# One more Strassen pair in the gate and up projections, their early sums taken once, and a third of the low halves made by an adding DMA

## The chip, the cores and the metric

The kernel runs on one core of a Trainium2 chip. The metric is the device time of one execution in microseconds (us), lower being better. TensorE (PE in the profile) multiplies, VectorE (DVE), ScalarE (ACT) and GpSimd (POOL) work on tiles in the on-chip memory, and SyncE (SP) issues the loads of the weights.

## The reference, cut to what matters

The reference is two transformer blocks in float32 on 256 tokens of width 2048, one after the other. The first has a differential attention beside a retention, a cross attention over 256 memory tokens, and a gated feed-forward part; the second has a gated spatial part beside a linear recurrence, and a convolved feed-forward part. The change touches the feed-forward part of the first block alone:

```
hf = rmsnorm(x, norm_ffn_g)                                    # (256, 2048)
x = x + (silu(hf @ w_gate) * (hf @ w_up)) @ w_down             # w_gate, w_up: (2048, 5632)
```

## The kernel before, in words

All products are made in three passes, since TensorE works on a shortened float32: each operand is written as hi + lo, where hi is the shortened value and lo the rest, and `mm3` (L190 to L195) issues hi·hi, hi·lo and lo·hi, three matmuls of 128x512. The helper `split` (L173) makes the two parts of a weight: ACT casts the raw weight `w` to `wh` (L175), DVE subtracts `wh` from `w` to get `wl` (L176).

Weights come from HBM in units of 1 MB (a tile `w` of 128x2048, three buffers, loaded by SP at L277). The list `seq` fixes the order of the units, `push` (L282) splits one piece of a unit, and `half` keeps up to five pieces split ahead of TensorE. The pieces `wh` and `wl` of 128x1024 have five buffers each, so a cast has to wait until TensorE has done with an older piece. The compiler of the language then sets the order of the instructions on each engine itself; the source fixes only what depends on what.

Gate and up are computed together by `gemm_q` (L413): 11 groups g of 512 columns, in three parts (PARTS: 4, 4 and 3 groups), each part followed by its share of `w_down`. The 2048 rows of the weights are 16 tiles of 128, taken as eight pairs; one unit `w` holds a pair for gate and up, four blocks of 128x512 (two of gate, then two of up in reversed order). With the tokens split in two halves of 128, one pair is a 2x2 by 2x2 product of blocks. KINDS says how each of the eight pairs u is computed:

- "N": eight products `mm3`, from two pieces (0 and 1) of 1024 columns. DVE makes one `wl` a piece.
- "S": seven products in Strassen's way (the variant of Winograd), from four pieces: "a" is the first half of the unit, "b" and "d" are sums of blocks that DVE makes first (L305 for "b"; L309 and L310 for "d"), "c" is the single block 2 of 512 columns, whose hi and lo go to ordinary tiles `r`.

Before, KINDS is "NSNSNSNN": three S pairs, five N pairs. The sums of the activations that S needs are made once for all groups by the class `Quad` (L103).

The products add up in seven banks of PSUM, M[1] to M[7]. M[2], M[3], M[4] and M[5] take the four buffers of the pool `pg`, M[1], M[6] and M[7] three of the four of the pool `pp`. M[1], M[6] and M[7] get products from S pairs alone. When no S pair is left, gemm_q calls `early` (L843): ACT copies M[1] to the tile m (L844), DVE adds M[6] to give u2 (L845) and M[7] to give u3 (L846). The call stands at the end of the loop over u (`if "S" not in ks[u + 1:]`), so with this KINDS it is made after u = 5, after u = 6 and after u = 7.

After a group, DVE takes the four banks out: M[2] + m (L853), M[4] + u3 (L855), M[5] twice (L857, L858), M[3] (L859); ACT applies SiLU to the first two (L854, L856), and L860 and L861 multiply. The next group needs the same four buffers, so its first products wait for these reads.

Of the kernel before, what the change touches and what calls it, by code (L numbers as in the profile page):

```python
# [8 lines left out]
F32 = mybir.dt.float32  # L9
F32R = mybir.dt.float32r  # L10
I32 = mybir.dt.int32
AF = mybir.ActivationFunctionType
ALU = mybir.AluOpType
# [4 lines left out]
S = 256  # L18
# [3 lines left out]
LN_EPS = 1e-5  # L22
LOOKAHEAD = 4
PARTS = [(0, 4), (4, 8), (8, 11)]
KINDS = "NSNSNSNN"
TAIL = 5


# [18 lines left out]
def tile_kernel(ctx, tc, x, xT, mem, memT, par, alibi, rdecay, ident_d, bc_rows, gm_wsT,  # L47
# [3 lines left out]
    V, A, T, G = nc.vector, nc.scalar, nc.tensor, nc.gpsimd  # L51
# [13 lines left out]
    def nm(s):  # L65
        cnt[0] += 1
        return f"{s}_{cnt[0]}"
# [4 lines left out]
    def rt():  # L72
        return tpool.tile([P, 2, S], F32R, tag="t", name=nm("r"))

    def flat(f):
        return f.rearrange("p a b -> p (a b)")
# [69 lines left out]
    def gps():  # L146
        return psg.tile([P, 512], F32, tag="g", name=nm("pg"))

    def sps():
        return pss.tile([P, 512], F32, tag="p", name=nm("pp"))  # L150
# [22 lines left out]
    def split(hi, lo, src, gcol=None):  # L173
        if gcol is None:
            A.copy(hi, src)  # L175
            V.tensor_tensor(lo, src, hi.bitcast(F32), ALU.subtract)  # L176
        else:
            A.activation(hi, src, AF.Identity, scale=gcol)
            V.scalar_tensor_tensor(lo, src, gcol, hi.bitcast(F32), ALU.mult, ALU.subtract)
# [11 lines left out]
    def mm3(out, lh, rh, start, stop):  # L191

        T.matmul(out, lhsT=lh[0], rhs=rh[0], start=start, stop=False)  # L193
        T.matmul(out, lhsT=lh[0], rhs=rh[1], start=False, stop=False)  # L194
        T.matmul(out, lhsT=lh[1], rhs=rh[0], start=False, stop=stop)  # L195
# [42 lines left out]
    seq = [(w_in_f, 0, u) for u in range(2)]  # L238
# [25 lines left out]
    def kind(w, u):  # L264
        return KINDS[u] if w is w_gu else "N"


    pieces = [(w, g, u, i) for w, g, u in seq for i in ((0, 1) if kind(w, u) == "N" else "acbd")]
    raws, last, sums = [], [None], {}

    def fetch():
        w, g, u = seq[pos[0]]
        raw = wraw.tile([P, 2048], F32, tag="w", name=nm("w"))
        n = 2 if pos[0] == 0 else 1
        for i in range(n):
            c = slice(2048 // n * i, 2048 // n * (i + 1))
            last[0] = nc.sync.dma_start(out=raw[:, c], in_=w[g, u][:, c])  # L277
        raws.append(raw)
        pos[0] += 1

    def push():

        w, g, u, i = pieces[pos[1]]
        if not raws:
            fetch()
        raw = raws[0]
        if i in (1, "d"):
            raws.pop(0)
        pos[1] += 1
        if pos[1] > len(pieces) - TAIL:  # L290

            hi, lo = [flat(rt()) for _ in range(2)], [flat(rt()) for _ in range(2)]
            for k in range(2):
                split(hi[k], lo[k], raw[:, 1024 * i + 512 * k:1024 * i + 512 * k + 512])
        else:
            if i == "c":
                hi, lo = flat(rt()), flat(rt())
            else:
                hi = whi.tile([P, 1024], F32R, tag="h", name=nm("wh"))
                lo = wlo.tile([P, 1024], F32R, tag="l", name=nm("wl"))  # L300
            b = raw.rearrange("p (b n) -> p b n", n=512)
            if i == "a":

                sums["b"] = wsum.tile([P, 2, 512], F32, tag="t", name=nm("wt"))
                V.tensor_tensor(sums["b"], b[:, 3:4, :].to_broadcast([P, 2, 512]), b[:, 0:3:2, :], ALU.subtract)  # L305
            if i == "c":

                d = sums["d"] = wsum.tile([P, 2, 512], F32, tag="t", name=nm("wt"))
                V.tensor_tensor(d[:, 0, :], sums["b"][:, 0, :], b[:, 2, :], ALU.subtract)  # L309
                V.tensor_tensor(d[:, 1, :], d[:, 0, :], b[:, 1, :], ALU.add)  # L310
            if i in ("b", "d"):
                src = sums.pop(i).rearrange("p b n -> p (b n)")
            else:
                src = raw[:, {0: slice(0, 1024), 1: slice(1024, 2048), "a": slice(0, 1024),
                              "c": slice(1024, 1536)}[i]]
            split(hi, lo, src)
        feed.append((w, g, u, i, hi, lo))

    def half(w, g, u, i, n):
# [11 lines left out]
    def tick():  # L331
        for g in list(bg):
            try:
                next(g)
            except StopIteration:
                bg.remove(g)
# [8 lines left out]
    def need(lst, i):  # L345
        while lst[i] is None:
            assert bg
            tick()
        return lst[i]
# [60 lines left out]
    def gemm_q(wap, g, acts, sums_done):  # L410

        M = [None] * 8
        n = len(acts)
        ks = [kind(wap, u) for u in range(n)]
        total = {m: sum(1 if k == "S" else 2 if m in (2, 3, 4, 5) else 0 for k in ks) for m in range(1, 8)}
        done = [0] * 8

        def prod(m, a, b):  # L420
            if M[m] is None:
                M[m] = gps() if m in (2, 3, 4, 5) else sps()
            done[m] += 1
            mm3(M[m], a, b, done[m] == 1, done[m] == total[m])

        for u in range(n):
            a = need(acts, u)
            if ks[u] == "N":
                plan = [(0, [(2, 0, 0, 0), (2, 0, 1, 1), (4, 1, 0, 0), (4, 1, 1, 1)]),
                        (1, [(5, 1, 1, 0), (5, 1, 0, 1), (3, "D", 1, 0), (3, "D", 0, 1)])]  # L430
                for i, ops in plan:
                    hi, lo = half(wap, g, u, i, 512)
                    for m, t, k, b in ops:
                        prod(m, a.diff(k) if t == "D" else a.blk(k, t), (hi[b], lo[b]))
                    tick()
            else:
                plan = [("a", [(1, a.blk(0, 0), 0), (2, a.blk(1, 0), 1)]),
                        ("c", [(3, a.sums(3), 0)]),
                        ("b", [(5, a.sums(0), 0), (7, a.sums(2), 1)]),
                        ("d", [(6, a.sums(1), 0), (4, a.blk(1, 1), 1)])]  # L440
                for i, ops in plan:
                    hi, lo = half(wap, g, u, i, 512)
                    for m, x, b in ops:
                        prod(m, x, (hi[b], lo[b]))
                    if i in "cd":
                        tick()
            if "S" not in ks[u + 1:]:
                sums_done(M)
        return M

    def evac_fm(ps, r):
# [29 lines left out]
    def add_x(ps, g):  # L481
        for t in range(2):
            V.tensor_tensor(xs(t, g), xs(t, g), ps[t], ALU.add)
# [329 lines left out]
    for g in range(4):  # L813
        add_x(gemm_tm(w_xo, g, xo), g)
        spawn(next_in(g, hf_a, sqf, cols("norm_ffn_g", 0, 16), None, KINDS), 1)

# [21 lines left out]
    for g0, g1 in PARTS:  # L838
        acts = [None] * (2 * (g1 - g0))
        for g in range(g0, g1):  # L840
# [7 lines left out]
            M = gemm_q(w_gu, g, hf_a, early)  # L848
# [236 lines left out]
    for g in range(2):  # L1085
        ps = gemm_tm(w_in2_t, g, h2_a)
        u = []
# [161 lines left out]
```

## Time and profile before

| what | value |
|---|---|
| time, median of 3 runs (lowest to highest) | 2601.64 us (2598.96 to 2602.27) |
| profiled execution, its time | 2601.45 us |
| its span, first to last instruction | 2599.7 us |
| mean granted clock of TensorE | 0.997 |
| DVE busy over the span | 69% |
| ACT busy over the span | 53% |
| POOL busy over the span | 2% |
| weight units of gate and up | 88, the first issued at 755.7 us, the last at 1418.9 us |
| DMA, mean over the span | 189 GB/s |

The profile's engine times are unions of busy time; a matmul is listed with its whole passage (0.39 us for 128x512), but the next one starts 0.22 to 0.23 us after it, so the distance of two starts says what a matmul costs. Groups are listed as: line, engine, operation, out<-in by the program's names, shapes, count, then busy time in all, mean ns of one, idle time of the engine before them. The view of the waits lists who waited for whom: us in total, times, longest.

### The profile page before, as it was taken

The numbers are of one execution on the slowest core, as the hardware profiler recorded it, in microseconds if no ns is written. First come the engines' busy times: TensorE is split into PE (matmuls) and PEld (weight loads), VectorE is DVE, ScalarE is ACT, GpSimd is POOL, SyncE is SP. The second block draws the span as 40 slices with busy tenths as digits, with TensorE's granted clock in tenths as the row PEclk, the third lists the DMA queues.
The fourth block names the chain that finished last, engine by engine and source line by source line (L and its number), as shares of the span: only waits on it lengthen the run. The fifth ranks groups of instructions, "written<-read, shape, count | busy, mean of one in ns | idle before, by whom it ended". The sixth has DMA issues, their size and how long they took to land.

```text
span 2599.7 us, 32474 instructions
## 1 busy us (share of the span) xinstructions
PE 2567.3 (99%) x12823; PEld 2172.7 (84%) x12823; DVE 1789.2 (69%) x2284; ACT 1381.7 (53%) x1882; POOL 39.0 (2%) x41
## 2 busy tenths in 40 slices
PE   8999999999999999999999999999999999999998
PEld 7888888888887878878887888888888888888887
DVE  7666566556579885888588767866777745777754
ACT  6555554454466553555355555755555534555543
POOL 1000010000000000000000000000000000000000
PEclk9999999999999999999999999999999999999999
DMA  7455555554454555455555555555555555555563
GB/s 257 162 179 211 201 201 189 194 178 162 146 188 168 196 193 194 178 206 196 193 182 180 205 208 192 178 192 181 188 185 193 184 193 192 194 185 188 189 213 132
DMA packets 72727, 490.58 MB, mean 189 GB/s; under 512 B 8192, under 2 KB 8320, under 8 KB 14592
## 3 DMA queue, kind: packets, MB, share of 16 engines
q1 hardware_dynamic: 72576, 488.52, 53.1%
q8 instruction: 100, 1.64, 0.2%
q14 instruction: 51, 0.42, 0.0%
HBM read 486.39 MB, written 2.10 MB: 188 GB/s over the span
## 4 chain that ended last, share of the span: by engine, by line
PE 94%; DVE 3%; issue 1%; ACT 1%; DMA 0%; SPq 0%; POOL 0%; ACTq 0%; POOLq 0%; DVEq 0%
PE pg L362 24%; PE pg L193 17%; PE pg L195 17%; PE pg L194 17%; PE pg L366 12%; PE pp L193 2%; PE pp L195 2%; PE pp L194 2%; DVE wl L176 1%; PE pp L186 1%; ACT wh L175 1%; DVE wt L305 0%; DVE f L845 0%; DVE f L846 0%; DMA w<-in_w_in_f_dram 0%
## 5 line engine op out<-in xcount | busy, mean ns | idle before, releaser
L176 DVE TENSOR_TENSOR wl<-w,wh 128x1024 fp32r<-128x1024 f32 x866 | 1059.6, 1225 | 665.7 <-ACT wh L175 662.0
L175 ACT CAST wh<-w 128x1024 fp32r<-128x1024 f32 x866 | 909.2, 1051 | 863.9 <-PE pg L195 583.9
L193 PE MATMUL pg<-wh,r 128*128 128x512 f32 x2059 | 798.6, 392 | 12.7 <-DVE f L855 11.2
L194 PE MATMUL pg<-wl,r 128*128 128x512 f32 x2059 | 804.6, 391 | 0.0
L195 PE MATMUL pg<-wh,r 128*128 128x512 f32 x2059 | 802.3, 390 | 0.0
L362 PE MATMUL pg<-r,wh 128*128 128x512 f32 x2688 | 714.9, 395 | 11.4 <-ACT wh L175 7.0
L362 PEld LDWEIGHTS pg<-r,wh 128*128 128x128 f32 x2688 | 471.0, 189 | 86.2 <-ACT wh L175 7.0
L193 PEld LDWEIGHTS pg<-wh,r 128*128 128x128 f32 x2059 | 387.2, 188 | 98.3 <-DVE f L855 14.7
L195 PEld LDWEIGHTS pg<-wh,r 128*128 128x128 f32 x2059 | 387.6, 188 | 80.7
L194 PEld LDWEIGHTS pg<-wl,r 128*128 128x128 f32 x2059 | 387.8, 188 | 80.4 <-DVE wl L176 1.1
L366 PEld LDWEIGHTS pg<-r,wl 128*128 128x128 f32 x2688 | 391.2, 190 | 41.7
L366 PE MATMUL pg<-r,wl 128*128 128x256 f32 x2688 | 406.0, 282 | 0.0
L454 ACT COPY f<-pg 128x256 f32<-128x256 f32 x168 | 60.7, 374 | 88.7 <-PE pg L362 88.7
L175 ACT CAST wh<-wt 128x1024 fp32r<-128x1024 f32 x66 | 69.6, 1055 | 55.3 <-DVE wt L310 21.2
L455 DVE TENSOR_TENSOR f<-pg,f 128x256 f32<-128x256 f32 x168 | 68.9, 420 | 43.7 <-ACT f L454 43.7
L176 DVE TENSOR_TENSOR wl<-wt,wh 128x1024 fp32r<-128x1024 f32 x66 | 80.3, 1219 | 11.9 <-ACT wh L175 11.2
L1112 DVE SCALAR_TENSOR_TENSOR f<-f,pr,f 128x255 f32<-128x255 f32 x192 | 79.9, 479 | 0.0
L456 DVE TENSOR_TENSOR f<-f,rows 128x512 f32<-128x512 f32 x84 | 58.1, 692 | 3.4 <-ACT rows L231 0.8
L1109 ACT ACTIVATE f<-f,pr 128x256 f32<-128x256 f32 x96 | 52.6, 594 | 12.6 <-DVE f L456 12.5
L175 ACT CAST r<-f 128x512 fp32r<-128x512 f32 (+1 forms) x72 | 43.0, 598 | 13.7 <-DVE f L456 8.7
L193 PE MATMUL pp<-wh,r 128*128 128x512 f32 x127 | 49.6, 395 | 0.0
L195 PE MATMUL pp<-wh,r 128*128 128x512 f32 x127 | 49.5, 390 | 0.0
(192 smaller groups left out, 1354.0 us busy)
## 6 DMA issues: line engine op xcount, KB each, us to landing
w<-in_w_up_dram SPq DMA_DIRECT2D x96, 1024.0 KB, 4.7
w<-in_w_down_dram SPq DMA_DIRECT2D x92, 1024.0 KB, 4.7
w<-in_w_gu_dram SPq DMA_DIRECT2D x88, 1024.0 KB, 4.8
w<-in_w_in_t_dram SPq DMA_DIRECT2D x40, 1024.0 KB, 4.8
w<-in_w_in_f_dram SPq DMA_DIRECT2D x39, 1024.0 KB, 4.7
w<-in_w_o_dram SPq DMA_DIRECT2D x16, 1024.0 KB, 4.8
w<-in_w_xk_dram SPq DMA_DIRECT2D x16, 1024.0 KB, 4.8
w<-in_w_xv_dram SPq DMA_DIRECT2D x16, 1024.0 KB, 4.7
```

Of the source, the lines that this page charges most:

```text
L175: A.copy(hi, src)
L176: V.tensor_tensor(lo, src, hi.bitcast(F32), ALU.subtract)
L193: T.matmul(out, lhsT=lh[0], rhs=rh[0], start=start, stop=False)
L194: T.matmul(out, lhsT=lh[0], rhs=rh[1], start=False, stop=False)
L195: T.matmul(out, lhsT=lh[1], rhs=rh[0], start=False, stop=stop)
L362: T.matmul(ps[m], lhsT=hi[k][:, m * P:(m + 1) * P], rhs=ops[k].both(k % 2), start=begin and k == 0, stop=stop, skip_group_check=True)
L366: T.matmul(ps[m][:, S:], lhsT=lo[k][:, m * P:(m + 1) * P], rhs=ops[k].hi(k % 2), start=False, stop=False, skip_group_check=True)
L454: A.copy(f[:, m, :], ps[m][:, S:])
L455: V.tensor_tensor(f[:, m, :], ps[m][:, 0:S], f[:, m, :], ALU.add)
L456: V.tensor_tensor(f, f, bc2(need(r, 0)), ALU.mult)
L1109: A.activation(y[:, j, :], z[:, j, :], AF.Identity, scale=col("ffn_conv_w_2", 192 + c), bias=col("ffn_conv_b_2", c))
L1112: V.scalar_tensor_tensor(y[:, j, d:], z[:, j, :S - d], col("ffn_conv_w_2", 96 * (2 - d) + c), y[:, j, d:], ALU.mult, ALU.add)
```

## The change

Four edits, all in the code of gate and up. The line numbers of the changed kernel are one higher from the constant ADDED on (`split` at L176 and L177, the sums at L306, L310 and L311) and six higher behind `push` (`early` at L850 to L852, taking out at L859 to L867).

1. KINDS goes from "NSNSNSNN" to "SNSNSNSN": a fourth pair is computed with seven products. The pairs S now stand first, and u = 0, 2, 4, 6.
2. The pieces of an S pair come in the order a, b, d, c instead of a, c, b, d. The raw unit is thus read until the last piece.
3. `early` is called only behind an S pair, so once in a group (after u = 6) instead of three times.
4. The second piece of the N pairs u = 1, 3, 5 (ADDED) gets its lo in another way: ACT casts hi, ACT then writes -hi to `wl`, and POOL issues a DMA that reads the same 512 KB of weights from HBM again and adds them onto `wl`. DVE does nothing for it. That is 33 adding DMAs, 3 in each of 11 groups.

```
-KINDS = "NSNSNSNN"
+KINDS = "SNSNSNSN"
+ADDED = (1, 3, 5)
...
-    pieces = [(w, g, u, i) for w, g, u in seq for i in ((0, 1) if kind(w, u) == "N" else "acbd")]
+    pieces = [(w, g, u, i) for w, g, u in seq for i in ((0, 1) if kind(w, u) == "N" else "abdc")]
...
-        if i in (1, "d"):
+        if i in (1, "c"):
             raws.pop(0)
...
-            if i == "c":
+            if i == "b":
                 d = sums["d"] = wsum.tile([P, 2, 512], F32, tag="t", name=nm("wt"))
...
-            split(hi, lo, src)
+            if i == 1 and w is w_gu and u in ADDED:
+                A.copy(hi, src)
+                A.activation(lo, hi.bitcast(F32), AF.Identity, scale=-1.0)
+                G.dma_start(out=lo, in_=w[g, u][:, 1024:2048], accum_op=ALU.add)
+            else:
+                split(hi, lo, src)
...
                 plan = [("a", [(1, a.blk(0, 0), 0), (2, a.blk(1, 0), 1)]),
-                        ("c", [(3, a.sums(3), 0)]),
                         ("b", [(5, a.sums(0), 0), (7, a.sums(2), 1)]),
-                        ("d", [(6, a.sums(1), 0), (4, a.blk(1, 1), 1)])]
+                        ("d", [(6, a.sums(1), 0), (4, a.blk(1, 1), 1)]),
+                        ("c", [(3, a.sums(3), 0)])]
...
-                    if i in "cd":
+                    if i in "bc":
                         tick()
-            if "S" not in ks[u + 1:]:
-                sums_done(M)
+                if "S" not in ks[u + 1:]:
+                    sums_done(M)
```

The first place is DVE at the end of the first group (g = 0), from the read of M[2] on; pg_1244 and pg_1245 are M[2] and M[4], pg_1248 is M[5]. Before:

```order
689 L853 TENSOR_TENSOR f_1323_7039<-pg_1244_6682,f_1239_6675 128x512
690 L845 TENSOR_TENSOR f_1240_6676<-pp_1278_6794,f_1239_6675 128x512
691 L310 TENSOR_TENSOR wt_1320_7014<-wt_1320_7014,w_1314_6992 128x512
692 L176 TENSOR_TENSOR wl_1329_7054<-wt_1317_6996,wh_1328_7053 128x1024
693 L846 TENSOR_TENSOR f_1241_6677<-pp_1274_6783,f_1240_6676 128x512
694 L176 TENSOR_TENSOR wl_1336_7081<-wt_1320_7014,wh_1335_7080 128x1024
695 L305 TENSOR_TENSOR wt_1351_7131<-w_1348_7127 128x1024
696 L855 TENSOR_TENSOR f_1324_7040<-pg_1245_6689,f_1241_6677 128x512
697 L857 TENSOR_TENSOR f_1240_6676<-pg_1248_6700,f_1240_6676 128x512
```

After, where pg_1245, pg_1255 and pg_1248 are M[2], M[4] and M[5]:

```order
690 L852 TENSOR_TENSOR f_1240_6675<-pp_1249_6699,f_1239_6674 128x512
691 L177 TENSOR_TENSOR r_1326_7028<-w_1316_6984,r_1325_7027 128x512
692 L859 TENSOR_TENSOR f_1329_7048<-pg_1245_6686,f_1238_6673 128x512
693 L306 TENSOR_TENSOR wt_1349_7102<-w_1346_7098 128x1024
694 L861 TENSOR_TENSOR f_1330_7049<-pg_1255_6715,f_1240_6675 128x512
695 L863 TENSOR_TENSOR f_1239_6674<-pg_1248_6695,f_1239_6674 128x512
696 L177 TENSOR_TENSOR wl_1324_7012<-wt_1322_7000,wh_1323_7011 128x1024
697 L177 TENSOR_TENSOR wl_1336_7065<-w_1334_7062,wh_1335_7064 128x1024
698 L864 TENSOR_TENSOR f_1240_6675<-pg_1248_6695,f_1240_6675 128x512
```

Between the reads of M[2] and M[4] stood six instructions, two of them the third run of the early sums, which M[4] + u3 has to follow; now there is one. The ends of the groups g = 2, 5 and 9 stood before as that of g = 0 did; after the change no group has more than two instructions between M[2] and M[4].

The second place is ACT at the end of the group g = 2, with the pieces of the next group behind it. Before:

```order
628 L844 COPY f_1401_7400<-pp_1421_7463 128x512
629 L175 CAST wh_1469_7699<-w_1468_7697 128x1024
630 L175 CAST wh_1480_7753<-wt_1471_7701 128x1024
631 L854 ACTIVATE f_1475_7739<-f_1475_7739,s_1322_7037 128x512
632 L175 CAST wh_1487_7780<-wt_1474_7719 128x1024
633 L856 ACTIVATE f_1476_7740<-f_1476_7740,s_1322_7037 128x512
```

After, where wh_1503 and wl_1504 are the second piece of the pair u = 1 of the next group:

```order
638 L176 CAST wh_1489_7730<-wt_1488_7719 128x1024
639 L176 CAST wh_1499_7778<-w_1498_7776 128x1024
640 L318 CAST wh_1503_7790<-w_1498_7776 128x1024
641 L860 ACTIVATE f_1493_7762<-f_1493_7762,s_1328_7046 128x512
642 L319 ACTIVATE wl_1504_7791<-wh_1503_7790 128x1024
643 L862 ACTIVATE f_1494_7763<-f_1494_7763,s_1328_7046 128x512
```

The early copies between the casts are gone, and between the cast of an added piece and its negation (L319), on which the DMA waits, stands the SiLU of the group that ends.

The third place is POOL, whose queue held 46 rows and holds 79; the rows of before around the first groups of gate and up:

```order
30 L199 TENSOR_TENSOR s_616_3124<-s_615_3122,mhalf_87 128x2
31 L199 TENSOR_TENSOR s_708_3662<-s_707_3659,mhalf_87 128x2
32 L199 TENSOR_TENSOR s_1322_7037<-s_1321_7034,mhalf_87 128x2
33 L955 AFFINE_SELECT f_2368_12212<-f_2368_12212 128x512
34 L955 AFFINE_SELECT f_2369_12213<-f_2369_12213 128x512
```

After:

```order
31 L200 TENSOR_TENSOR s_708_3662<-s_707_3659,mhalf_87 128x2
32 L320 DMA wl_1247_6691<-in_w_gu_dram 128x1024
33 L200 TENSOR_TENSOR s_1328_7046<-s_1327_7043,mhalf_87 128x2
34 L320 DMA wl_1283_6817<-in_w_gu_dram 128x1024
35 L320 DMA wl_1299_6896<-in_w_gu_dram 128x1024
```

The 33 DMAs stand one behind the other, with one small power (the rsqrt of the norm of hf) between the first and the second.

TensorE's order changes in every group too. Counted in it, from the matmul that frees the buffer of an added piece's `wh` to the first matmul that reads its `wl`, there stand 30 matmuls for the pair u = 1 of g = 1, 33 for that of g = 2, 3 and 7, 38 for that of g = 6 and 10, and 44 to 53 for the other 27 added pieces.

## The prediction

> **What bounds the kernel now.** I read the page's head first, then who waited for whom on TensorE, then the stages of gate and up by windows and by groups, and last the DMA issues.
>
> ```profile
> span 2599.7 us, 32474 instructions
> ...
> PE 2567.3 (99%) x12823; PEld 2172.7 (84%) x12823; DVE 1789.2 (69%) x2284; ACT 1381.7 (53%) x1882; POOL 39.0 (2%) x41
> ```
>
> TensorE is busy for 2567.3 of 2599.7 us, so time comes off only where it has fewer matmuls or fewer pauses. In the stretch of gate and up and their w_down (755 to 1450 us), the list of TensorE's waits begins with this line; four pauses of up to 3.1 us wait for L855, the read of M[4]:
>
> ```profile
> PE pg L193 <- DVE f L855: 11.2, 4, 3.1
> ```
>
> The windows of two whole groups without such a pause, g = 1 to 2 and g = 4 to 5 (the columns are the window, its length, busy us and instructions of PE, PEld, DVE, ACT, POOL, granted clock, DMA share, GB/s):
>
> ```profile
> 866.90:910.40 43.50, 43.10 (x192) 34.68 (x191) 39.33 (x46) 24.95 (x29) 0.00 (x0) 1.00 0.54 192
> 1085.40:1128.90 43.50, 43.15 (x192) 34.75 (x191) 39.33 (x46) 25.00 (x30) 0.00 (x0) 1.00 0.53 190
> ```
>
> TensorE sets these groups, but DVE has 39.33 of 43.5 us, 90%: there is little room, and its order decides. How a pause comes about stands in DVE's time line at the end of g = 0:
>
> ```profile
> 819.49 0.68 DVE L853 TENSOR_TENSOR f<-pg,f 128x512 f32<-128x512 f32 x1
> 820.09 0.68 DVE L845 TENSOR_TENSOR f<-pp,f 128x512 f32<-128x512 f32 x1
> 820.69 0.68 DVE L310 TENSOR_TENSOR wt<-wt,w 128x512 f32<-128x512 f32 x1
> 821.29 1.22 DVE L176 TENSOR_TENSOR wl<-wt,wh 128x1024 fp32r<-128x1024 f32 x1
> 822.43 0.68 DVE L846 TENSOR_TENSOR f<-pp,f 128x512 f32<-128x512 f32 x1
> 823.24 1.22 DVE L176 TENSOR_TENSOR wl<-wt,wh 128x1024 fp32r<-128x1024 f32 x1
> 824.38 1.22 DVE L305 TENSOR_TENSOR wt<-w 128x1024 f32<-128x1024 f32 x1
> 825.52 0.68 DVE L855 TENSOR_TENSOR f<-pg,f 128x512 f32<-128x512 f32 x1
> ```
>
> M[2] is out at 820.2, M[4] only at 826.2: between them lie the third run of the early sums (L845, L846) and 4.3 us of work for the next S pair. The next group needs M[4]'s bank after its first six matmuls.
>
> **The change part by part.** The profiled execution took 2601.45 us (span 2599.7 and 1.75 around it); the median of the runs is 2601.64, so the sum against the one holds for the other.
>
> *Four S pairs for three.* An S pair has 7 products for 8, so 11 groups x 1 product x 3 = 33 matmuls go. What one costs is the distance of two starts, not its 0.39 us; and that distance doubles for a while after a pause, as TensorE's time line at the end of g = 9 shows:
>
> ```profile
> 1394.29 0.39 PE L194 MATMUL pg<-wl,r 128*128 128x512 f32 x1
> 1394.52 0.39 PE L195 MATMUL pg<-wh,r 128*128 128x512 f32 x1
> 1397.62 0.79 PE L193 MATMUL pg<-wh,r 128*128 128x512 f32 x1 [2.71 <-DVE f L855]
> 1398.21 0.63 PE L194 MATMUL pg<-wl,r 128*128 128x512 f32 x1
> 1398.64 0.63 PE L195 MATMUL pg<-wh,r 128*128 128x512 f32 x1
> ```
>
> The first two start 0.23 us apart, the last two 0.43. With 12 us / 54 = 0.222 (below) I take 0.225: 33 x 0.225 = 7.4 us gained.
>
> *Early sums once.* In each group the second and third runs go: on DVE 2 x (0.684 + 0.683) = 2.7 us, on ACT 2 x 0.577 = 1.2 us. The pauses are the point. Since M[4] + u3 no longer follows a last run of L846, the read of M[4] stands at most two instructions behind that of M[2] in every group of the changed order. At up to 1.22 us each (L305 and L176 in the time line) M[4] is out within 3.2 us of M[2]'s end, where it took 6.0. Late next is M[5], whose second read stands two low halves further (0.68 + 2 x 1.22 + 0.68 = 3.8 us), but its bank is needed later as well, as the new group's third. So I let the four pauses go whole. Their price, with the slowed matmuls behind them, is what TensorE missed in 12 us around each, against 12 undisturbed us of w_down (last row):
>
> ```profile
> 820.00:832.00 12.00, 8.91 (x32) 0.86 0.35 134
> 911.00:923.00 12.00, 9.29 (x41) 1.00 0.40 151
> 1130.00:1142.00 12.00, 9.29 (x42) 1.00 0.36 130
> 1392.00:1404.00 12.00, 9.29 (x28) 0.72 0.39 142
> 1005.00:1017.00 12.00, 12.00 (x54) 1.00 0.55 197
> ```
>
> 22 + 13 + 12 + 26 = 73 matmuls are missing, x 0.222 = 16.2 us: 11.2 of pause and 5.0 of halved clock, 1.25 a pause.
>
> *DVE's and ACT's load.* The groups of the gate and up stretch:
>
> ```profile
> L176 DVE TENSOR_TENSOR wl<-w,wh 128x1024 fp32r<-128x1024 f32 x221 | 269.2, 1221 | 127.9 <-ACT wh L175 126.7
> L175 ACT CAST wh<-w 128x1024 fp32r<-128x1024 f32 x221 | 232.5, 1054 | 235.4 <-PE pg L195 224.8 <-PE pp L195 7.5 <-DMA w<-in_w_gu_dram 1.4
> L305 DVE TENSOR_TENSOR wt<-w 128x1024 f32<-128x1024 f32 x33 | 40.2, 1218 | 2.4 <-DMA w<-in_w_gu_dram 2.4
> L845 DVE TENSOR_TENSOR f<-pp,f 128x512 f32<-128x512 f32 x33 | 22.6, 684 | 1.0 <-PE pp L195 0.7
> L846 DVE TENSOR_TENSOR f<-pp,f 128x512 f32<-128x512 f32 x33 | 22.5, 683 | 0.0
> L310 DVE TENSOR_TENSOR wt<-wt,w 128x512 f32<-128x512 f32 x33 | 22.5, 682 | 0.0
> L175 ACT CAST r<-w 128x512 fp32r<-128x512 f32 x33 | 20.0, 620 | 14.8 <-DMA w<-in_w_gu_dram 14.8
> L844 ACT COPY f<-pp 128x512 f32<-128x512 f32 x33 | 19.1, 577 | 0.1
> L856 ACT ACTIVATE f<-f,s 128x512 f32<-128x512 f32 x11 | 7.9, 722 | 17.3 <-DVE f L855 17.3
> L854 ACT ACT_TABLE_LOAD x1 | 1.3, 1283 | 0.7 <-DVE f L853 0.7
> ```
>
> For DVE an S pair costs 1.22 + 3 x 0.68 + 3 x 1.22 = 6.9 us (its three sums, the low half of "c" at 0.68, three of 1.22), an N pair 2 x 1.22 = 2.4. The fourth S adds 4.5, the three adding DMAs take off 3 x 1.22 = 3.7, the early sums 2.7: 1.9 us less, 37.4 of some 42.8 us. ACT gets 1.7 for the S pair (3 x 1.05 + 0.62 - 2 x 1.05) and 3 x 1.05 for the negations (priced as a cast), less 1.2: 28.6 of 42.8. I cost the other edits at nothing: c's raw unit is held some 3 us longer, but a unit lands 4.8 us after its issue and three buffers cover about two pairs, 10 us.
>
> *The adding DMAs.* Here is the unknown. No such DMA is in this trace. An added piece's way is: buffer free, cast 1.05, negation 1.05, DMA of X us, first matmul that reads `wl`. Time for X is the matmuls in between (counted in the changed order) x 0.225, less ACT's work. For u = 1 of g = 2, 3, 7: 33 x 0.225 = 7.4 less two casts and the SiLU's 0.72 gives 4.6 us; of g = 6 and 10 (38 matmuls) 5.7; of g = 1 (30 matmuls, and ACT's table load and another cast between) 1.5. Of the other 27, four have 6.4, six 7.1, the rest 7.6 to 9.2. What X may be:
>
> ```profile
> w<-in_w_gu_dram SPq DMA_DIRECT2D x88, 1024.0 KB, 4.8
> f<-in_xT_dram SPq DMA_DIRECT2D x8, 256.0 KB, 8.4
> pr<-in_par_dram SPq DMA_DIRECT2D x1, 8.0 KB, 1.7
> ```
>
> 1.7 us hold nearly without bytes, and 1 MB adds 3.1. If only the 512 KB read from HBM count, X is 1.7 + 1.55 = 3.3; if the `wl` that is added to is read as well, it moves as much as a unit, 4.8. Weight units hold the DMA engines for 0.54 of the time, so a collision adds up to 3.1: 7.9; the slowest small DMA, issued in a crowd, took 8.4, and I take this as the upper end, with POOL's own issuing, which no row shows, inside it. My value is 4.8 and half a collision, 6.4. A POOL queue with one DMA in some 14 us delays nobody behind it.
>
> The Trainium skill (Collectives: The Full Stack, section "The bandwidth ceiling: the fold count and why AG ≠ RS ≠ AR") says that an add in the DMA engines is not slower for the adding, but reads two sources at half the rate. No run here shows that yet; without collisions the sum would be 2583 by it and 2580 by the bytes of the weights alone.
>
> Summed over the 33 pieces, TensorE waits 1.7 us at X = 3.3, 4.0 at 4.8, 12.0 at 6.4 (4.9 in g = 1, 3 x 1.8, 2 x 0.7, 4 x 0.05), 32.5 at 7.9 (21 of 33 late), 43.5 at 8.4. A pause of 3 us or more costs 1.25 of clock besides: one at 6.4, four at 7.9, six at 8.4. The term is 13.2 us, between 1.7 and 51.
>
> Sum: 2601.45 - 7.4 - 16.2 + 13.2 = 2591.
>
> **The rivals.**
>
> *The adding DMAs land later than 7.2 us* (slower). From there the term is over 23.6 and eats the gain; the place is TensorE's second matmul of a product, waiting for `wl`. At 7.9 the sum is 2615, at 8.4 2629. For it: casting an added piece frees its raw unit, so the next load starts just before the adding DMA and the two collide. Against it: the engines idle for 46% of the time.
>
> *They land early* (X up to 4.8): 2580 to 2583. For it: nothing but the plain rows; against it the same collision.
>
> *The pauses stay.* S pairs now end and begin a group: over u = 6, 7, 0, 1 DVE has 6.9 + 2.4 + 6.9 + 1.2, 6.3 for the early sums and the banks (nine instructions of about 0.7) and 1.4 for two low halves of transposed tiles, 25 us, TensorE 90 x 0.225 = 20. If the five pieces split ahead don't bridge that, nothing of the 16.2 comes: 2607. Against it: before, the five pairs around the end (S, three N, S) held 13.8 + 7.2 + 6.3 + 2.7 + 1.4 = 31 us against 114 x 0.225 = 26, and seven of eleven ends passed.
>
> *POOL can't issue while DVE is busy.* DVE's line above has no gap from 819.49 to 826; if each issue waited for one, 3 us on average by half of that run, X = 9.4: 71 us of waiting, ten clock losses, 2662. The Trainium skill (SBUF — State Buffer, section "SBUF: two separate sides") knows such a hold for DMAs issued from GpSimd, under DVE's two-port modes; its section "Who interferes with whom" gives TENSOR_TENSOR, all that DVE's rows here show, no such mode, so by that rule it would not come.
>
> **How the numbers follow.** Forecast (X from 4.8 to 7.2, pauses gone) 0.50: 2583 to 2602; early landing 0.14; late landing 0.19; pauses stay 0.12; POOL held 0.05. A measurement of this kernel can tell about 0.2%, 5.2 us, from no change. Faster by more: 0.43 of the forecast and 0.14, 0.57. Within: 0.07 of the forecast, 0.05 of the staying pauses, 0.04 of late landing, 0.16. Slower: 0.27. The range leaves out the lowest early landings, most of late landing beyond 8.1 and the held POOL, under 0.2: 2578 to 2622. The forecast's own is 2583 to 2602.
>
> **What would show it.** In the profile after: TensorE's waits without the read of M[4] (now L861), and no other read of a bank in its place; the early lines 11 times each; adding DMAs 33 times with a median landing near 6.4, and TensorE waiting for them mainly at u = 1 of g = 1, 2, 3 and 7; DVE near 37 us a group. The prediction is wrong if the landings are over 7.2, if TensorE waits for DVE at the ends of groups as before, or if pauses appear outside gate and up.

## The result and the profile after

The changed kernel takes 2618.87 us (median of 4 runs, 2614.7 to 2620.88) beside 2601.95 us for the kernel before (4 runs): ratio 1.0063, 95% interval 1.0046 to 1.0081. It is slower by about 17 us. The prediction said 2591 us, faster: the wrong side, inside its range. The profiled execution took 2620.88 us.

The head of the page of the changed kernel:

```profile
span 2619.2 us, 32539 instructions
...
PE 2569.8 (98%) x12790; PEld 2170.4 (83%) x12790; DVE 1772.9 (68%) x2265; ACT 1412.8 (54%) x1915; POOL 69.4 (3%) x74
```

There are 33 matmuls fewer, as the change says, and TensorE is nevertheless busy 2.5 us longer (2567.3 before) and idle 17.0 us longer (2619.2 - 2569.8 = 49.4, before 32.4). The 33 matmuls should have taken 33 x 0.225 = 7.4 us of busy time with them; matmuls that are slower for a while after a pause are counted as busy time too.

Who waited for whom on TensorE in 755 to 1450 us of the changed kernel (us in total, times, longest):

```profile
PE pg L195 <- DMA wl<-in_w_gu_dram: 17.3, 10, 3.5
PE pp L194 <- ACT wh L176: 7.2, 6, 1.6
PE pg L194 <- DVE f L859: 3.2, 3, 1.5
PE pg L195 <- DVE wl L177: 1.9, 2, 1.1
```

The wait for the read of M[4] (L861 now, 11.2 us in four places before) is gone, as forecast. In its place stand the adding DMAs and, which the prediction did not have, hi parts that ACT casts late and three shorter pauses at the read of M[2] (L859). Why ACT is late stands in its own list of waits, and DVE has the same wait (one line of each view, the changed kernel):

```profile
ACT wh L176 <- DMA w<-in_w_gu_dram: 38.6, 14, 3.5
```

```profile
DVE wt L306 <- DMA w<-in_w_gu_dram: 37.7, 20, 3.8
```

Before, these were 1.4 and 2.4 us. ACT also waits for units at the cast of c, 14.8 us before and 10.6 now; together its waits for units go from 16.2 to 49.2 us. The ordinary weight units come late. The DMA issues on the page (KB each, median us from issue to landing):

```profile
w<-in_w_gu_dram SPq DMA_DIRECT2D x88, 1024.0 KB, 5.3
...
wl<-in_w_gu_dram POOLq DMA_DIRECT2D x33, 512.0 KB, 7.4
```

An adding DMA lands after 7.4 us in the median (prediction 6.4, crossing point 7.2), and a unit needs 5.3 for 4.8. Two groups of the changed kernel, from one end to the next (window, its length, busy us and instructions of PE, PEld, DVE, ACT, POOL, granted clock, DMA share, GB/s):

```profile
871.10:918.50 47.40, 43.19 (x184) 34.92 (x185) 38.62 (x45) 27.38 (x32) 2.59 (x3) 0.96 0.68 211
1093.80:1141.60 47.80, 45.74 (x201) 36.10 (x199) 38.36 (x46) 29.30 (x33) 2.59 (x3) 1.00 0.68 209
```

An undisturbed group took 43.5 us before; these two take 47.4 and 47.8, with DVE near the load that was forecast (38.5 for 37.4) and TensorE no longer filled. Over the eight groups that follow another one within a part, from the read of M[2] to the next such read, the mean goes from 44.8 us (42.4 to 47.5) to 47.0 (45.6 to 48.3).

### The profile page after: what moved, and what is told of

It is laid out like the page before. It is cut to its first block, busy times and chain, and to the rows that moved or that the text cites. A ratio compares the mean times of both kernels' runs of the same rounds, so it can differ in the third digit from the quotient of the medians.

```text
span 2619.2 us, 32539 instructions
## 1 busy us (share of the span) xinstructions
PE 2569.8 (98%) x12790; PEld 2170.4 (83%) x12790; DVE 1772.9 (68%) x2265; ACT 1412.8 (54%) x1915; POOL 69.4 (3%) x74
## 3 DMA queue, kind: packets, MB, share of 16 engines
q0 software_dynamic: 4752, 17.30, 3.7%
## 4 chain that ended last, share of the span: by engine, by line
PE 88%; DMA 6%; DVE 2%; ACT 2%; issue 1%; POOL 0%; SPq 0%; ACTq 0%; POOLq 0%; DVEq 0%
PE pg L368 24%; PE pg L195 16%; PE pg L196 16%; PE pg L194 15%; PE pg L372 12%; DMA wl<-in_w_gu_dram 3%; DMA w<-in_w_gu_dram 3%; PE pp L195 1%; PE pp L196 1%; PE pp L194 1%; DVE wl L177 1%; PE pp L187 1%; ACT wh L176 1%; ACT wh L318 0%; ACT wl L319 0%
## 5 line engine op out<-in xcount | busy, mean ns | idle before, releaser
L177 DVE TENSOR_TENSOR wl<-w,wh 128x1024 fp32r<-128x1024 f32 x822 | 1006.0, 1225 | 652.8 <-ACT wh L176 649.2
L176 ACT CAST wh<-w 128x1024 fp32r<-128x1024 f32 x822 | 862.3, 1051 | 825.5 <-PE pg L196 504.6
L195 PE MATMUL pg<-wl,r 128*128 128x512 f32 x2004 | 787.4, 393 | 19.4 <-DMA wl<-in_w_gu_dram 17.3
L196 PE MATMUL pg<-wh,r 128*128 128x512 f32 x2004 | 784.5, 392 | 0.0
L194 PE MATMUL pg<-wh,r 128*128 128x512 f32 x2004 | 773.5, 392 | 3.2 <-DVE f L859 3.2
L194 PEld LDWEIGHTS pg<-wh,r 128*128 128x128 f32 x2004 | 377.8, 189 | 81.9 <-DVE f L859 4.4
L196 PEld LDWEIGHTS pg<-wh,r 128*128 128x128 f32 x2004 | 378.8, 189 | 78.6
L372 PEld LDWEIGHTS pg<-r,wl 128*128 128x128 f32 x2688 | 391.1, 190 | 41.8
L176 ACT CAST wh<-wt 128x1024 fp32r<-128x1024 f32 x88 | 91.7, 1050 | 72.3 <-DVE wt L311 48.7
L177 DVE TENSOR_TENSOR wl<-wt,wh 128x1024 fp32r<-128x1024 f32 x88 | 105.9, 1219 | 11.8 <-ACT wh L176 11.4
L461 DVE TENSOR_TENSOR f<-pg,f 128x256 f32<-128x256 f32 x168 | 68.9, 419 | 43.7 <-ACT f L460 43.7
L306 DVE TENSOR_TENSOR wt<-w 128x1024 f32<-128x1024 f32 x44 | 53.7, 1221 | 38.1 <-DMA w<-in_w_gu_dram 37.7
L194 PE MATMUL pp<-wh,r 128*128 128x512 f32 x160 | 64.3, 403 | 7.2 <-ACT wh L176 7.2
L195 PE MATMUL pp<-wl,r 128*128 128x512 f32 x160 | 63.0, 394 | 0.1
L196 PE MATMUL pp<-wh,r 128*128 128x512 f32 x160 | 62.8, 392 | 0.0
```

The lines of the kernel that those rows point to most:

```text
L372: T.matmul(ps[m][:, S:], lhsT=lo[k][:, m * P:(m + 1) * P], rhs=ops[k].hi(k % 2), start=False, stop=False, skip_group_check=True)
L461: V.tensor_tensor(f[:, m, :], ps[m][:, 0:S], f[:, m, :], ALU.add)
```

## The experiments

Edits are numbered as in the section on the change: 1 the fourth S pair, 2 the order a, b, d, c, 3 the early sums once, 4 the adding DMAs. "To before" is the median less the median of the kernel before, run on the same chip beside it (2600.4 to 2602.67 us); an interval is some 4 us wide to either side for the shorter series and 2 for the longer. The expectations were written from the bare medians, so that their differences are up to 1.1 us off those used here.

| run | S pairs | order | adding DMAs on | us | to before | ratio, 95% interval |
|---|---|---|---|---|---|---|
| e2_early_once | 3 | a, c, b, d | none | 2579.21 | -21.7 | 0.9914 (0.9899 to 0.9930) |
| e6_three_new_order | 3 | a, b, d, c | none | 2579.98 | -22.0 | 0.9916 (0.9903 to 0.9930) |
| e7_three_old_add | 3 | a, c, b, d | 0, 2, 4 | 2598.85 | -3.1 | 0.9989 (0.9980 to 0.9998) |
| e3_three_pairs | 3 | a, b, d, c | 0, 2, 4 | 2589.28 | -11.6 | 0.9953 (0.9940 to 0.9965) |
| e5_order_no_add | 4 | a, c, b, d | none | 2581.65 | -20.3 | 0.9923 (0.9910 to 0.9937) |
| e11_one_add | 4 | a, c, b, d | 3 | 2578.78 | -21.6 | 0.9917 (0.9903 to 0.9931) |
| e4_old_order | 4 | a, c, b, d | 1, 3, 5 | 2602.07 | +1.2 | 1.0003 (0.9994 to 1.0012) |
| e1_no_add | 4 | a, b, d, c | none | 2604.75 | +3.9 | 1.0014 (1.0005 to 1.0022) |
| e8_plain_copy | 4 | a, b, d, c | 1, 3, 5, as plain copies | 2599.08 | -2.9 | 0.9991 (0.9982 to 1.0000) |
| the changed kernel | 4 | a, b, d, c | 1, 3, 5 | 2618.87 | +16.9 | 1.0063 (1.0046 to 1.0081) |
| e9_c_early | 4 | a, b, d, c; c split with b | none | 2587.62 | -15.1 | 0.9945 (0.9932 to 0.9959) |
| e12_c_before_b | 4 | a, b, d, c; c split before b | none | 2587.02 | -13.4 | 0.9949 (0.9934 to 0.9963) |
| e10_c_early_add | 4 | a, b, d, c; c split with b | 1, 3, 5 | 2593.91 | -8.8 | 0.9963 (0.9950 to 0.9975) |

All of them have edit 3. Diffs are against the changed kernel.

**Without the adding DMAs (e1_no_add).**

```
-ADDED = (1, 3, 5)
+ADDED = ()
```

> The changed kernel with ADDED = (): four S pairs, early sums once, no adding DMA; DVE makes all low halves. Theory A (the adding DMAs cost the time: they land at a median of 7.4 us, and the weight loads beside them land later): the waits for wl and most of the late units go, 2578 to 2590 us. Theory B (the raw unit is held longer by the order a, b, d, c, so units come late): the waits for units stay, 2605 to 2620. Theory C (DVE is too full with four S pairs): DVE has 3.7 us more in a group, about 41 of 43, and the time rises to 2620 or more.

Without a single adding DMA the kernel is still slower than before, by 3.9 us. (The time is just under the 2605 to 2620 us of theory B.) So the rival on which most of the prediction's doubt lay, late adds, is at most 13.1 us of what is lost; something else had eaten the whole gain. TensorE's waits in e1 (755 to 1450 us), and below them one line each of ACT's and DVE's:

```profile
PE pp L194 <- ACT wh L176: 6.6, 6, 1.9
PE pp L195 <- DVE wl L177: 3.5, 5, 0.9
```

```profile
ACT wh L176 <- DMA w<-in_w_gu_dram: 52.8, 15, 5.0
```

```profile
DVE wt L306 <- DMA w<-in_w_gu_dram: 33.3, 20, 3.1
```

The units are late without any adding DMA, and land in 4.8 us as before: they are issued late.

**Only the early sums (e2_early_once).** The kernel before with edit 3 alone: three S pairs, the old order, no adds. Its diff against the kernel before:

```
-            if "S" not in ks[u + 1:]:
-                sums_done(M)
+                if "S" not in ks[u + 1:]:
+                    sums_done(M)
```

> The kernel before with one edit alone: the early sums are taken once, behind the last S pair. If the four pauses at the read of M[4] came from the repeated sums, as the prediction has it, they go whole: 2602 - 16 = 2586 us, with no wait for that read over 1 us. The rival (the ends of groups are short of DVE anyway and the pauses only move to another bank): 2598 to 2602.

21.7 us are gained by this edit alone. In gate and up TensorE waits for nothing that the view of waits lists; a group is all TensorE (page head, then a window of one group):

```profile
span 2577.2 us, 32402 instructions
...
PE 2559.1 (99%) x12823; PEld 2172.4 (84%) x12823; DVE 1764.0 (68%) x2240; ACT 1369.4 (53%) x1860; POOL 39.3 (2%) x41
```

```profile
860.10:902.50 42.40, 42.40 (x193) 35.19 (x192) 37.55 (x44) 23.98 (x27) 0.00 (x0) 1.00 0.56 199
```

Against before, with the same 12823 matmuls, 8.2 us of busy time are gone (most of it matmuls slowed after a pause) and 14.3 of idle time.

**Three S pairs, with the adds, in either order (e3_three_pairs, e7_three_old_add) and without them in the new order (e6_three_new_order).**

```
-KINDS = "SNSNSNSN"
-ADDED = (1, 3, 5)
+KINDS = "NSNSNSNN"
+ADDED = (0, 2, 4)
```

(This is e3; e6 has ADDED = (), and e7 the order "acbd" besides.)

> The changed kernel with KINDS as before (three S pairs, NSNSNSNN) and ADDED = (0, 2, 4): early sums once and 33 adding DMAs, but no fourth S pair. Theory A: the adding DMAs still land at 6 to 8 us and TensorE or the units still wait for them, 2600 to 2615 us, 15 to 30 over the same kernel without them (early sums once alone). Theory C: with DVE relieved by 3.7 us a group and no fourth pair it is the fastest, 2585 or less.

> Three S pairs, early sums once, the pieces in the new order a, b, d, c, no adding DMA. Theory B: units come late with three pairs too, but there is more slack: 2583 to 2592 us, over the 2579 of the old order. Theory C (the number of pairs, not the order): 2578 to 2581.

> Three S pairs, early sums once, the old order, and the adding DMAs at u = 0, 2, 4. Theory A (the adding DMAs are late by themselves and slow the loads beside them, whatever the order): 2586 to 2595 us, against 2579 without them. Rival (they hurt only where the raw unit is held long): 2579 to 2583.

With three pairs the new order costs nothing (-22.0 for -21.7), and the adds cost 18.6 us in the old order and 10.4 in the new. Both theories for e3 and for e7 missed: e3 lies between its two, and e7, at 2598.85 us, above both of its.

**The old order with four pairs, with and without adds (e4_old_order, e5_order_no_add).**

```
-for i in ((0, 1) if kind(w, u) == "N" else "abdc")]
+for i in ((0, 1) if kind(w, u) == "N" else "acbd")]
...
-                        ("d", [(6, a.sums(1), 0), (4, a.blk(1, 1), 1)]),
-                        ("c", [(3, a.sums(3), 0)])]
+                        ("d", [(6, a.sums(1), 0), (4, a.blk(1, 1), 1)])]
```

(with "c" second in the plan; e5 has ADDED = () besides.)

> The changed kernel with the pieces of an S pair in the order of before (a, c, b, d), so that the raw unit is free after the second piece. Theory A: the adding DMAs collide with the unit loads as before, 2610 to 2622 us, at most 6 off the changed kernel. Theory B: the units come in time again, 2595 to 2605, and the waits of DVE L306 for the unit, 37.7 us in the changed kernel, fall under 10.

> Four S pairs, early sums once, the pieces in the old order a, c, b, d, no adding DMA. Theory B (the new order holds the raw unit to the last piece, and the S pair's first sum needs a whole unit): the late units, 33 us of DVE's and 53 of ACT's waits in the run without adds and with the new order, go, and the fourth pair brings its 33 matmuls: 2571 to 2580 us. Theory C (DVE is full with four pairs): TensorE still waits for low halves and sums, 2590 to 2605.

e5 differs from e1 in edit 2 alone: -20.3 for +3.9. The order that the prediction priced at nothing costs 24.2 us with four pairs and no adds. With the adds it costs 15.7 (the changed kernel against e4); in e4 DVE's waits for units at its first sum fell from 37.7 to 23.9 us, not under 10 as theory B expected. And e5 differs from e2 in edit 1 alone, by which the S pairs also move from u = 1, 3, 5 to u = 0, 2, 4, 6: 1.4 us, nothing that can be told, where 7.4 were to be gained. TensorE's waits in e5, and two groups:

```profile
PE pg L195 <- DVE wl L177: 2.5, 4, 1.1
PE pp L194 <- ACT wh L176: 1.8, 1, 1.8
```

```profile
862.50:906.20 43.70, 43.56 (x195) 35.20 (x194) 42.67 (x49) 26.18 (x30) 0.00 (x0) 1.00 0.57 205
1076.60:1120.30 43.70, 43.70 (x198) 36.18 (x198) 41.66 (x49) 25.37 (x30) 0.00 (x0) 1.00 0.55 199
```

With four pairs and no adds DVE is busy for 42.67 and 41.66 of 43.7 us. These two are the longest groups of e5: counted as above, from read to read of M[2], its eight groups take 41.8 to 43.7 us, 42.7 in the mean, and those of e2, with one product more, 41.8 to 42.4, mean 42.2. DVE is nearly full, and 2.5 of TensorE's 4.3 us of waits are for its low halves. That DVE sets the group is not shown by this: TensorE is busy nearly all through both windows, and e11 (below), which takes one low half of 1.2 us in each group off DVE, is not faster by anything that can be told.

**Plain copies for the adds (e8_plain_copy).** The DMAs go out at the same places with the same bytes and the same waits, but overwrite `wl` instead of adding to it, so that the lo halves of those pieces are the weights themselves.

```
-                G.dma_start(out=lo, in_=w[g, u][:, 1024:2048], accum_op=ALU.add)
+                G.dma_start(out=lo, in_=w[g, u][:, 1024:2048])
```

> The changed kernel with the adding DMA made a plain one: it writes the weights over wl instead of adding them, so the low halves of these pieces are wrong and the product with them too; all waits and bytes read from HBM are the same. If an add takes twice a copy's time since it reads two sources, the packets take half as long, the median landing falls from 7.4 to 5 or 6 us and the time by 5 to 15 us. If the fixed cost of a DMA from POOL is what makes it late, the landing stays over 6.5 and the time within 5 us of the changed kernel.

19.8 us go with the word "add". The share of the 16 DMA engines' time that the queue takes in 755 to 1450 us (packets, MB, share), the changed kernel first, then e8:

```profile
q0 software_dynamic: 4752, 17.30, 14.0%
```

```profile
q0 software_dynamic: 4752, 17.30, 7.9%
```

The same 4752 packets hold the engines 1.77 times as long when they add: 0.140 x 16 x 695 / 4752 = 0.328 us a packet in the mean, against 0.185 us. (The 17.30 MB are 4224 packets of 4 KB; the other 528 carry next to nothing, so that a packet of 4 KB takes somewhat more than the mean in both.) The copies land in 5.8 us for 7.4, the units in 4.8 for 5.3:

```profile
w<-in_w_gu_dram SPq DMA_DIRECT2D x88, 1024.0 KB, 4.8
...
wl<-in_w_gu_dram POOLq DMA_DIRECT2D x33, 512.0 KB, 5.8
```

With copies the kernel is even 6.8 us faster than with none of these DMAs (e1). The likely reason, not tried by itself, is that DVE is relieved of 33 low halves (busy 1772.8 us for 1807.2). So the adds' 13.1 us are 19.8 for the adding less a relief of 6.8.

**c split together with b (e9_c_early, e10_c_early_add).** The products keep the new order, but the raw unit's last read is in its second piece again. The tiles of c are held two pieces longer.

```
             if i == "c":
-                hi, lo = flat(rt()), flat(rt())
+                feed.append((w, g, u, i) + sums.pop("c"))
+                return
...
+            if i == "b":
+                sums["c"] = flat(rt()), flat(rt())
+                split(*sums["c"], raw[:, 1024:1536])
```

> Four pairs by Strassen, the new order of the products (a, b, d, c), no adding DMAs, as in e1 (2604.75 us, ratio 1.0014); the one difference: c's hi/lo split is made together with b's, so that the raw unit's last read is at its second piece again, as in the old order, and c's two tiles are held two pieces longer. Theory 'the raw unit is held too long' (the 23 us between e5 and e1 are units that are issued late because a buffer is read until the fourth piece): the time falls to e5's, 2578 to 2586 us, ratio about 0.992, and VectorE's waits of the first sum for a unit, 33.3 us in 20 places in e1, fall to about e5's 8.6. Theory 'the order of the products itself' (the products of d wait for sums, or the later c shifts the combination of the products): 2599 to 2606 us, with those waits still 25 us or more.

> The changed kernel as it is, with its adding DMAs on 1, 3, 5, and the same one difference as e9: c's split together with b's. Theory 'the raw unit is held too long': e9's time and what the adds cost with four pairs in the old order (20.4 us, e4 against e5), or with the new (14.1 us): 2592 to 2604 us, and the median landing of the adds stays at 7 us or more. Theory 'the order of the products itself': 2614 to 2622 us, as the changed kernel. Were the late units also what makes the adds late (both are queued behind each other's data), the adds' price falls under 9 us and the time under 2592.

e9 is 18.9 us faster than e1, of the 24.2 us that edit 2 cost. How a unit that is read too long delays the next shows in DVE's time line of e1, reduced to the first sum of an S pair (L306) and the low half of c (`r<-w`):

```profile
870.47 1.22 DVE L306 TENSOR_TENSOR wt<-w 128x1024 f32<-128x1024 f32 x1
...
881.07 1.21 DVE L306 TENSOR_TENSOR wt<-w 128x1024 f32<-128x1024 f32 x1
...
895.25 1.28 DVE L177 TENSOR_TENSOR r<-w,r 128x512 fp32r<-128x512 f32 x2
...
899.49 1.23 DVE L306 TENSOR_TENSOR wt<-w 128x1024 f32<-128x1024 f32 x1 [2.96 <-DMA w<-in_w_gu_dram]
```

The c of both pairs, whose sums began at 870.47 and 881.07, are finished side by side at 895.25. Until then two of the three raw buffers are held; the next S unit can't be there when DVE wants it at 896.5. In e9 (time line of the same stretch) the c's come one by one; that at 884.77 is of the pair before, those of 876.15, 890.78 and 897.06 are done at 890.18, 893.05 and 900.47, and the next first sum waits 0.98 us:

```profile
876.15 1.22 DVE L307 TENSOR_TENSOR wt<-w 128x1024 f32<-128x1024 f32 x1
...
884.77 0.68 DVE L177 TENSOR_TENSOR r<-w,r 128x512 fp32r<-128x512 f32 x1
...
890.18 0.68 DVE L177 TENSOR_TENSOR r<-w,r 128x512 fp32r<-128x512 f32 x1
890.78 1.22 DVE L307 TENSOR_TENSOR wt<-w 128x1024 f32<-128x1024 f32 x1
...
897.06 1.23 DVE L307 TENSOR_TENSOR wt<-w 128x1024 f32<-128x1024 f32 x1 [0.98 <-DMA w<-in_w_gu_dram]
```

From DVE's first sum to its last read of the unit, over all 44 S units, the mean is 10.2 us in e5 and 13.1 in e1; but the longest is 18.9 in e5, and 26.9 in e1, where nine units are held 25 us and more. The waits of ACT's casts and of DVE's first sum for a unit fall from 52.8 and 33.3 us in e1 to (e9):

```profile
ACT wh L176 <- DMA w<-in_w_gu_dram: 14.7, 11, 3.1
```

```profile
DVE wt L307 <- DMA w<-in_w_gu_dram: 17.8, 12, 2.7
```

With the casts of c counted in, ACT's waits for units fall from 61.5 to 28.9 us, near e5's 26.3. DVE's stay at twice e5's 8.6, to which they were expected to fall.

The theory that the raw unit is held too long gave 2578 to 2586 for e9; 2587.62 is just outside, and 5.3 us of edit 2 stay. e10, the changed kernel with this one repair, is 25.7 us faster than the changed kernel, and its adds cost 6.3 us, less than the 13.1 without it, though they land no earlier (7.8 us for 7.4):

```profile
PE pg L195 <- DMA wl<-in_w_gu_dram: 12.4, 11, 3.1
PE pp L194 <- ACT wh L176: 0.6, 1, 0.6
```

Little but the waits for the adds is left. The expectation that earlier units would also bring the adds in earlier has failed.

**c split before b, and one add in place of three (e12_c_before_b, e11_one_add).** e12 is e9 with c's split ahead of b's; e11 is e5 with `ADDED = (3,)`.

> As e9 (four pairs, the new order of the products, no adds, c's split made with b's; 2587.62 us, ratio 0.9945), but c's split is made before b's own, so that the splits come in the old order a, c, b, d and only the products keep the new. Theory 'the rest of the 23 us (6 us) is the products' order': unchanged, 2585 to 2590 us. Theory 'it is the order of the splits on ScalarE and VectorE': e5's time, 2579 to 2584 us.

> Four pairs, the old order of pieces and products, early sums once, as in e5 (2581.65 us, ratio 0.9923), and one adding DMA in place of three: the lo half of unit 3 in each of the eleven groups. Theory 'each add costs its late landing by itself, where its piece is due' (three cost 20.4 us, e4 against e5, so 33 adds at 0.62 us): 11 adds cost 6 to 8 us, 2588 to 2590 us, and TensorE waits for the piece that the DMA adds to in places. Theory 'it is the traffic of three adds on top of eight units' (adds that collide with unit loads and with each other): one add lands at 6 us or less, delays no unit, and takes 1.3 us of VectorE work a group off an engine that TensorE waits for in e5: 2574 to 2582 us.

e12 stays at e9's time, so the last 5 to 7 us of edit 2 belong to the order of the products (or to c's tiles, which both runs hold longer) and not to that of the splits. Both runs have a pause of 2.7 to 2.9 us for a bank at the start of a group that e5 does not have (TensorE's waits in e12, L862 being the read of M[2]):

```profile
PE pg L194 <- DVE f L862: 3.3, 2, 2.7
```

Which of the products has to stand where to avoid it was not tried. In e11 one add per group does no harm, though it lands late:

```profile
PE pg L195 <- DMA wl<-in_w_gu_dram: 0.2, 1, 0.2
```

```profile
wl<-in_w_gu_dram POOLq DMA_DIRECT2D x11, 512.0 KB, 8.7
```

It costs nothing (-21.6 for e5's -20.3, not to be told apart), where a third of three adds' 21.5 us would have been 7. So adds do not cost by the piece. But the theory of the traffic, whose time came true, expected the lone add to land at 6 us or less, and its median of 8.7 us is the latest of all runs. A late landing costs only where TensorE comes to the piece before it. In e4, with the same order and three adds, TensorE's 15.3 us of waits for them belong to u = 1 with 6.8 us, to u = 3 with 1.4 and to u = 5 with 7.1 (each wait counted for the add issued last before it that had 3 us or more to land): e11 kept the add that cost least. Whether a lone add at u = 1 or u = 5 would be as cheap, and so whether place or traffic decides, was not tried.

e11 and e2 are the fastest found, 2578.78 and 2579.21 us, both 0.8% faster than the kernel before and 1.5% faster than the changed one; between them nothing can be told. A fourth raw buffer, the plainest cure for edit 2, was not tried.

## Why the prediction was wrong, point by point

The 16.9 us come apart along e2, e5, e1 and the changed kernel: -21.7 for the early sums, +1.4 for the fourth pair, +24.2 for the order, +13.1 for the adds. The prediction's sum was -16.2, -7.4, 0 and +13.2.

- *Early sums once, -16.2.* Right, and mis-sized: -21.7 (interval -18 to -26). All four pauses went, and e2 shows 14.3 us less idle time for the 11.2 summed and 8.2 us of busy time for the 5.0 of halved clock. The sum counted only the four long pauses. Of the rest of the idle time, 1.3 us were four short waits for casts of ACT in the same stretch and the others lay outside it.
- *The fourth pair, -7.4.* The failed step of this term is that 33 matmuls fewer shorten the stage by their own time. They went, and e5 is no faster than e2. Of the 7.4 us, 5.8 came back as idle time (23.9 for 18.1; 4.3 of it are the waits for low halves and a hi above), and the busy time fell by only 3.6 (2555.5 us for 2559.1). It is not the clock: nowhere in gate and up of e5 do the matmuls start 0.43 us apart. The term's own working had DVE at 37.4 + 3.7 = 41.1 us a group without the adds; e5 shows 41.7 to 42.7 in groups of 43.7, so that TensorE had little room left in which to gain. That DVE's load is the whole reason is not shown. With the adds, which relieve DVE, the fourth pair gains nothing either: e4 is 4.3 us slower than e7 (old order; the adds stand on other pairs).
- *The other edits "at nothing".* This is the step that put the forecast on the wrong side. "c's raw unit is held some 3 us longer" was right on average (13.1 for 10.2 us). "Three buffers cover about two pairs, 10 us" was not: c's split is the last piece of its unit, and it waits behind the casts and the tiles of the pieces ahead of it, so that two units were held together, up to 27 us. A mean holding time does not say whether a ring of three covers it; the longest one says more. With three pairs the same order is free (e6): the cost is that of edits 1 and 2 together, and neither shows it alone. Why three pairs bear it and four do not stays open. DVE's load (37.5 us in a group of e2, some 42 in e5) can't be the whole reason: in e8 DVE is busy for 1772.8 us, near e6's 1766.7, and its first sums still wait 34.0 us for units. The S pairs also stand closer: over the end of a group KINDS puts three N units between two S units with three pairs, and one with four. Neither was tried by itself.
- *The adding DMAs, +13.2.* The net, 13.1, agrees, but by luck and not by the working: over the five kernels that were run with and without three adds the price goes from 6.3 to 21.5 us. They land at 7.4 us, beyond the crossing point, where the table interpolates to some 29 us (13.2 at 6.4; 32.5 and four clock losses, 37.5, at 7.9); against that DVE's relief, which the sum gave no price, brings 6.8. The place was wrong too. Forecast was u = 1 of g = 1, 2, 3 and 7. The long waits, 2.1 to 3.5 us, stand 11 to 14 us ahead of the read of M[2] that ends a group, where u = 5 is computed. One of them, in the chain of the changed kernel's waits:

```profile
1209.98 0.48 ACT r L176
1210.46 0.96 ACT wl L319
1211.42 0.28 issue
1211.70 10.80 DMA wl<-in_w_gu_dram
1222.50 0.04 issue
1222.55 0.67 PE pg L195
```

and SP's queue beside it:

```profile
1210.35 2.65 SPq L278 DMA_DIRECT2D w<-in_w_gu_dram  x2
1213.28 8.28 SPq L278 DMA_DIRECT2D w<-in_w_down_dram  x2
```

Four units of 1 MB are issued within 11 us around it, one just before the adding DMA goes out at 1211.70 and two within 1.6 us behind it; the add lands after 10.8 us. "Half a collision" on top of 4.8 us left out that an add can meet a burst of units. The working has a slip besides: by its own times four pauses reach 3 us at X = 8.4, not six, so that this end of the term is 2.5 us lower.

- *The doubled source.* The prediction gave X without collisions as 4.8 if the tile added to is read as well, and 3.3 if not. e8 decides for the first: 0.328 us a packet for 0.185, and the earliest landings were 5.4 us for an add and 3.9 for a copy. The Trainium skill (Collectives: The Full Stack, section "The bandwidth ceiling: the fold count and why AG ≠ RS ≠ AR") says of the add in a ReduceScatter that it needs two source reads and so runs at about half the rate of a copy; the 1.77 here comes near that.
- *The rivals.* "Land later than 7.2 us" is what the median shows, and the sign is its sign. But by its table a landing of 7.4 us gave some 2607, not 2619, and it is not what turned the gain into a loss: without any add the kernel is at 2604.75 us, and with the late units mostly mended (e10) the adds, at 7.8 us, cost 6.3. "The pauses stay" is out as it was put: no wait for L861 is left. But the sign that no other read of a bank takes its place did not come: L859 is waited for, 3.2 us in three places. "POOL can't issue while DVE is busy" is out: POOL's 33 issues took 0.86 us each with DVE busy.

What stays open: what ate the fourth pair's gain, why the new order is free with three pairs, which pause of the new order of products makes the last 5 to 7 us, and why the adds cost 18.6 to 21.5 us in the old order and 6.3 to 13.1 in the new.

## What to carry to other kernels

When an edit lengthens the last read of a buffer, look for the longest holding time in the ring, with the queue ahead of that read, and not for the mean; and look at it in the kernel with all the other edits, since a stage that has slack for one of them may have none for two. Work taken off TensorE is not gained where another engine has come near its limit in the same stage: 33 matmuls less were worth nothing here with DVE at some 42 of 43.7 us, so the busy time of the next engine, per group and for the changed kernel, belongs in the sum. A landing time alone prices no DMA: one add in a group landed last of all, at 8.7 us, and cost nothing. Of the four edits here one alone was worth more than all of them: try them apart.

## What the runs showed of the hardware

A DMA that adds from HBM onto on-chip memory took 1.77 times the engine time of the same copy, and its landing of 7.4 us was 5.8 for the copy; units of 1 MB in the runs with adds took 5.1 to 6.3 us in the median instead of 4.8, and 4.8 beside the plain copies.

TensorE's clock fell after a shorter pause than the 3 us of the prediction. The changed kernel's time line around a wait of 2.52 us:

```profile
809.20 0.39 PE L194 MATMUL pp<-wh,r 128*128 128x512 f32 x1
812.10 0.50 PE L195 MATMUL pg<-wl,r 128*128 128x512 f32 x1 [2.52 <-DMA wl<-in_w_gu_dram]
...
813.13 0.63 PE L196 MATMUL pg<-wh,r 128*128 128x512 f32 x1
813.56 0.63 PE L195 MATMUL pg<-wl,r 128*128 128x512 f32 x1
```

Four matmuls behind the wait the starts are 0.43 us apart for 0.23. The Trainium skill (TensorE: Matmul & The Clock Gate, section "What's actually happening") gives an idle window of about 3.4 us for this; here 2.9 us from start to start were enough, and the measurement decides.
